# A row mean over 64 MB: the last row of each partition in three pieces instead of two

## The chip, the core and the metric

One core of a Trainium2 chip runs the kernel alone. The metric is the time of one execution on the device in microseconds (us); the median of the runs is what counts. Besides, one execution is recorded by the hardware profiler. Its span, from the first profiled instruction to the last, is a little shorter than the time, since some work lies around it.

The engines that matter here: VectorE (DVE), ScalarE (ACT) and GpSimd (POOL) compute; SyncE (SP) issues DMAs; 16 DMA engines move the data. A semaphore of a DMA is raised by each of the 16 engines, so a transfer counts as landed when the last of them is done.

## The reference

```python
def reference(x: np.ndarray, divisor: float) -> np.ndarray:
    return (np.sum(x, axis=-1) / divisor).astype(np.float32)
```

`x` is 32 x 512 x 1024 in float32 (67.1 MB), `divisor` is 1024. So 16384 rows of 1024 numbers are each summed and scaled by 1/1024.

## The kernel before

The 16384 rows lie on 128 partitions, 128 rows on each. They go in three groups: the first 16 rows of each partition (`x_first`), 96 rows (`x_main`), and the last 16 (`x_last`). Each load brings some rows of all partitions, one contiguous run per partition, and every load is issued from SP in the order of the program (`load`, L181, L182). The bulk loads of 14, 12 or 9 rows rotate through three buffers `t`, so a load waits until DVE has finished with the buffer it goes into.

- First and main group (L197 to L207): DVE sums the rows of a buffer in one reduction (L205). In the last two loads of the group ACT takes 4 and 5 of the rows (`act_sum`, L184 to L186). POOL then scales all sums (L207).
- Last group (L208 to L218): 9, 4 and 2 rows, in `t`, `t4` and `t2`. Here `dve_mean` (L188 to L195) is used: it adds the second half of a row to the first, scales, and accumulates the result along the row, in one pass of half the width. The accumulated value is written by a second small instruction, the accumulator read (DVE_READ_ACCUMULATOR2_ANT). ACT takes 4, 2 and 1 of these rows.
- The last row comes in two halves of 512 columns, `pa` and `pb` (L219, L220). `dve_mean` of `pa` (L226) writes its sum into column 512 of `pb`, behind the 512 columns that the DMA brings. Column 513 is zero: POOL clears columns 512 and 513 early (L179). `dve_mean` of `pb` (L227) then runs over 514 columns, that is 257 wide, takes the carried sum along, scales by 1/1024 and writes the last column of `fin`. So the second half waits for the first one's sum, through a semaphore of DVE itself, and for its own DMA.

The stores: `res0` (L223) and `res` (L224) are issued on SP behind all loads; `fin` (L228) last. Three functions work on the finished program. `start_loads_at_once` puts the loads that wait for nothing (the first three) ahead of the start barrier. `latest_wait_first` orders the waits of an instruction so that the wait for a DMA stays on the instruction itself, while the others become semaphore waits (EVENT_SEMAPHORE) of their own in front of it. `close_while_storing` moves the store of `fin` into the closing part of the program: it is issued once the last DVE result is there (semaphore `landed`), and the closing barrier of the engines runs while it is under way.

Each DMA counts on one of eight semaphores in turn, and its issue waits for the transfer that last used the same one.

Of the kernel before, what the change touches and what calls it, by code (L numbers as in the profile page):

```python
# [9 lines left out]
F32 = mybir.dt.float32  # L10
# [115 lines left out]
@with_exitstack  # L126
def kernel(
    ctx: ExitStack,
    tc: tile.TileContext,
    x: bass.AP,  # L130
    divisor: float,
    out: bass.AP,
):
    nc = tc.nc
    landed = nc.alloc_semaphore("landed")
    nc.at_finalize(start_loads_at_once)
    nc.at_finalize(latest_wait_first)
    nc.at_finalize(lambda nc: close_while_storing(nc, landed))
    xf = x.flatten_outer_dims()
    N, D = xf.shape  # L140
    P = nc.NUM_PARTITIONS
    scale = 1.0 / float(divisor)
    J = N // P
    assert J * P == N


    F, L = 16, 16
    M = J - F - L
    W = M + L
    x_first = bass.AP(tensor=x.tensor, offset=0, ap=[[F * D, P], [D, F], [1, D]])  # L150
    x_main = bass.AP(tensor=x.tensor, offset=P * F * D, ap=[[W * D, P], [D, M], [1, D]])
    x_last = bass.AP(tensor=x.tensor, offset=P * F * D + M * D, ap=[[W * D, P], [D, L], [1, D]])
    o_first = bass.AP(tensor=out.tensor, offset=0, ap=[[F, P], [1, F]])
    o_main = bass.AP(tensor=out.tensor, offset=P * F, ap=[[W, P], [1, M]])
    o_last = bass.AP(tensor=out.tensor, offset=P * F + M, ap=[[W, P], [1, L]])


    first = [(2, 0), (14, 0)]
    main = [(14, 0)] * 5 + [(14, 4), (12, 5)]
    last = [(9, 4), (4, 2), (2, 1)]  # L160
    assert sum(n for n, _ in first) == F
    assert sum(n for n, _ in main) == M and sum(n for n, _ in last) == L - 1

    pad = ctx.enter_context(tc.tile_pool(name="pad", bufs=1))
    pad.tile([P, 224], F32, name="pad")
    bulk = ctx.enter_context(tc.tile_pool(name="bulk", bufs=3))
    one = ctx.enter_context(tc.tile_pool(name="one", bufs=1))
    psum = ctx.enter_context(tc.tile_pool(name="junk", bufs=4, space=bass.MemoryType.PSUM))


    c = 512
    t4 = one.tile([P, 4, D], F32, name="t4")
    t2 = one.tile([P, 2, D], F32, name="t2")
    pa = one.tile([P, 768], F32, name="pa")[:, :c]
    pb = one.tile([P, D - c + 16], F32, name="pb")[:, : D - c + 2]
    res0 = one.tile([P, F], F32, name="res0")
    res = one.tile([P, M], F32, name="res")
    fin = one.tile([P, L], F32, name="fin")
    nc.gpsimd.memset(pb[:, D - c :], 0.0)  # L179

    def load(dst, src):  # L181
        tc.keep_in_program_order(nc.sync.dma_start(out=dst, in_=src))  # L182

    def act_sum(dst, src, by=1.0):  # L184
        junk = psum.tile([P, D], F32, name="junk")
        nc.scalar.activation(junk, src, COPY, scale=by, accum_out=dst)  # L186

    def dve_mean(dst, src, by=scale):  # L188


        h = src.shape[-1] // 2
        nc.vector.tensor_tensor_reduce(  # L192
            out=src[:, :h], in0=src[:, :h], in1=src[:, h:], scale=by, scalar=0.0,
            op0=ADD, op1=ADD, accum_out=dst,
        )  # L195

    for loads, src, dst in ((first, x_first, res0), (main, x_main, res)):  # L197
        j = 0
        for rows, on_act in loads:
            t = bulk.tile([P, 14, D], F32, name="t")  # L200
            load(t[:, :rows, :], src[:, j : j + rows, :])
            d = rows - on_act
            for i in range(d, rows):
                act_sum(dst[:, j + i : j + i + 1], t[:, i, :])
            nc.vector.reduce_sum(out=dst[:, j : j + d], in_=t[:, :d, :], axis=AX)  # L205
            j += rows
        nc.gpsimd.tensor_scalar_mul(out=dst, in0=dst, scalar1=scale)  # L207
    j = 0  # L208
    for rows, on_act in last:
        t = bulk.tile([P, 14, D], F32, name="t")[:, :rows, :] if rows > 4 else t4 if rows == 4 else t2  # L210
        load(t, x_last[:, j : j + rows, :])
        d = rows - on_act
        for i in range(rows):
            if i < d:
                dve_mean(fin[:, j + i : j + i + 1], t[:, i, :])
            else:
                act_sum(fin[:, j + i : j + i + 1], t[:, i, :], by=scale)
        j += rows  # L218
    load(pa, x_last[:, j, :c])  # L219
    load(pb[:, : D - c], x_last[:, j, c:])  # L220


    tc.keep_in_program_order(nc.sync.dma_start(out=o_first, in_=res0))  # L223
    tc.keep_in_program_order(nc.sync.dma_start(out=o_main, in_=res))  # L224

    dve_mean(pb[:, D - c : D - c + 1], pa, by=1.0)  # L226
    dve_mean(fin[:, j:], pb)  # L227
    tc.keep_in_program_order(nc.sync.dma_start(out=o_last, in_=fin))  # L228


# [33 lines left out]
```

## Time and profile before

| what | us |
|---|---|
| time, median of 3 runs | 160.5 (160.44 to 160.51) |
| span of the profiled execution | 159.0 |
| DVE busy | 117.2 |
| ACT busy | 18.5 |
| end of the load of `t2` (2 rows), by what waits for it | 155.86 |
| issue of the store of `fin` | 157.56 |

The span is the time between the first and the last profiled instruction. The kernel reads 67.11 MB, at 422 GB/s as a mean over the span. DVE waits 34.0 us in front of the reductions of L205, in each case for a DMA. "PEq", "SPq" and the like are an engine's sequencer, which waits, branches and issues while the engine itself does nothing.

### The profile page before, as it was taken

To read this page: it belongs to the slowest core of one execution; us is meant where nothing else is said; L and a number is where in the kernel's file an instruction comes from. 1 tells how busy PE (TensorE), PEld (TensorE's weight loads), DVE (VectorE), ACT (ScalarE), POOL (GpSimd) and SP (SyncE) were. 2 spreads that over 40 slices of the span, in tenths; PEclk is the share of its full clock that TensorE was granted. 3 is DMA by queue.
4 is the path that set the end of the run, shared out by engine and by line. 5 is a ranking of instruction groups with operands and counts; after the bars stand their busy time and mean duration, and the time that the engine had idled before them with its cause. 6 is when DMAs were issued, how large, how long until landed. Compare 5 with 4: busy or idle time off the path is not lost.

```text
span 159.0 us, 148 instructions
## 1 busy us (share of the span) xinstructions
DVE 117.2 (74%) x29; ACT 18.5 (12%) x33; POOL 1.0 (1%) x7
## 2 busy tenths in 40 slices
DVE  0500059995999599978999599959995996395643
ACT  3000000000000000000000000000000900390684
POOL 0000000000000000000000000000000000001000
DMA  7999999959999999699999999699999999999894
GB/s 278 447 462 462 462 462 462 462 260 433 462 462 462 462 462 462 303 390 462 462 462 462 462 462 404 303 447 462 462 462 429 396 396 408 482 445 445 350 420 169
DMA packets 2448, 67.18 MB, mean 422 GB/s; under 512 B 656, under 2 KB 656, under 8 KB 912
## 3 DMA queue, kind: packets, MB, share of 16 engines
q1 hardware_dynamic: 2448, 67.18, 98.3%
HBM read 67.11 MB, written 0.07 MB: 422 GB/s over the span
## 4 chain that ended last, share of the span: by engine, by line
DMA 77%; DVE 21%; SPq 1%; issue 0%; DVEq 0%
DMA t<-in_x_dram 56%; DMA pb<-in_x_dram 21%; DVE res L205 20%; SPq L182 1%; DVE pb L192 0%; DVEq L259 0%
## 5 line engine op out<-in xcount | busy, mean ns | idle before, releaser
L205 DVE TENSOR_REDUCE res<-t 128x14 f32<-128x14336 f32 (+3 forms) x9 | 111.2, 12360 | 34.0 <-DMA t<-in_x_dram 34.0
L186 ACT ACTIVATE junk<-t 128x1024 f32<-128x1024 f32 x16 | 16.2, 1013 | 136.8 <-DMA t<-in_x_dram 136.8
L192 DVE CUSTOM_DVE_ANT_0 t<-t 128x512 f32<-128x512 f32 x8 | 5.1, 688 | 6.1 <-DMA t<-in_x_dram 6.1
L186 ACT ACTIVATION_READ_ACCUMULATOR junk<-t 128x1 f32 x16 | 3.0, 186 | 0.0
L207 POOL TENSOR_SCALAR res<-res 128x16 f32<-128x16 f32 (+1 forms) x2 | 0.7, 352 | 143.3 <-DVE res L205 143.3
L186 ACT ACT_TABLE_LOAD x1 | 1.3, 1283 | 1.7 <-PEq L245 1.7
L192 DVE DVE_READ_ACCUMULATOR2_ANT fin<- 128x1 f32 x9 | 0.7, 82 | 0.0
L192 DVE CUSTOM_DVE_ANT_0 pb<-pb 128x257 f32<-128x257 f32 x1 | 0.4, 428 | 0.2 <-DMA pb<-in_x_dram 0.2
L192 DVE CUSTOM_DVE_ANT_0 pa<-pa 128x256 f32<-128x256 f32 x1 | 0.4, 426 | 0.0
L179 POOL MEMSET pb<- 128x2 f32 x1 | 0.1, 99 | 1.3 <-POOLq L245 1.3
L245 POOL MEMSET const-bfloat16-1.0<- 128x1 bf16 x1 | 0.1, 101 | 0.0
L245 POOL MEMSET const-uint8-127<- 128x1 uint8 x1 | 0.1, 101 | 0.0
L245 POOL MEMSET const-float32-0.0<- 128x1 f32 x1 | 0.1, 98 | 0.2 <-issue 0.2
L245 POOL MEMSET const-float32-1.0<- 128x1 f32 x1 | 0.1, 98 | 0.0
L192 DVE DVE_READ_ACCUMULATOR2_ANT pb<- 128x1 f32 x1 | 0.1, 84 | 0.0
## 6 DMA issues: line engine op xcount, KB each, us to landing
t<-in_x_dram SPq DMA_DIRECT2D x7, 7168.0 KB, 35.6
t<-in_x_dram SPq DMA_DIRECT2D x1, 6144.0 KB, 33.3
t<-in_x_dram SPq DMA_DIRECT2D x1, 4608.0 KB, 27.2
t<-in_x_dram SPq DMA_DIRECT2D x2, 1024.0 KB, 19.2
t<-in_x_dram SPq DMA_DIRECT2D x1, 2048.0 KB, 31.7
pa<-in_x_dram SPq DMA_DIRECT2D x1, 256.0 KB, 33.8
pb<-in_x_dram SPq DMA_DIRECT2D x1, 256.0 KB, 33.9
out_dram<-res SPq DMA_DIRECT2D x1, 48.0 KB, 11.6
```

Of the source, the lines that this page charges most:

```text
L179: nc.gpsimd.memset(pb[:, D - c :], 0.0)
L182: tc.keep_in_program_order(nc.sync.dma_start(out=dst, in_=src))
L186: nc.scalar.activation(junk, src, COPY, scale=by, accum_out=dst)
L192: nc.vector.tensor_tensor_reduce(out=src[:, :h], in0=src[:, :h], in1=src[:, h:], scale=by, scalar=0.0, op0=ADD, op1=ADD, accum_out=dst,)
L205: nc.vector.reduce_sum(out=dst[:, j : j + d], in_=t[:, :d, :], axis=AX)
L207: nc.gpsimd.tensor_scalar_mul(out=dst, in0=dst, scalar1=scale)
L245: nc = _bacc.Bacc("TRN2", target_bir_lowering=False, num_devices=1)
```

## The change

The last row comes in three loads, of 384, 352 and 288 columns (1536, 1408 and 1152 bytes per partition). `dve_mean` of a piece writes its sum behind the columns of the next one, so there are two carried sums instead of one. The widths on DVE become 192, 177 (half of 352 + 2) and 145 (half of 288 + 2). POOL clears two pairs of columns. The tiles are 2048 bytes per partition each, in place of one of 3072 and one of 2112; `t`, `t4` and `t2` keep their places.

```diff
-    c = 512
+    cuts = ((0, 384), (384, 736), (736, D))
     t4 = one.tile([P, 4, D], F32, name="t4")
     t2 = one.tile([P, 2, D], F32, name="t2")
-    pa = one.tile([P, 768], F32, name="pa")[:, :c]
-    pb = one.tile([P, D - c + 16], F32, name="pb")[:, : D - c + 2]
+    pieces = [
+        one.tile([P, 512], F32, name=f"piece{k}")[:, : hi - lo + 2 * (k > 0)]
+        for k, (lo, hi) in enumerate(cuts)
+    ]
...
-    nc.gpsimd.memset(pb[:, D - c :], 0.0)
+    for piece, (lo, hi) in zip(pieces[1:], cuts[1:]):
+        nc.gpsimd.memset(piece[:, hi - lo :], 0.0)
...
-    load(pa, x_last[:, j, :c])
-    load(pb[:, : D - c], x_last[:, j, c:])
+    for piece, (lo, hi) in zip(pieces, cuts):
+        load(piece[:, : hi - lo], x_last[:, j, lo:hi])
...
-    dve_mean(pb[:, D - c : D - c + 1], pa, by=1.0)
-    dve_mean(fin[:, j:], pb)
+    for piece, after, (lo, hi) in zip(pieces, pieces[1:], cuts[1:]):
+        dve_mean(after[:, hi - lo : hi - lo + 1], piece, by=1.0)
+    dve_mean(fin[:, j:], pieces[-1])
     tc.keep_in_program_order(nc.sync.dma_start(out=o_last, in_=fin))
```

In the built program the order of all other instructions is as before on every engine. DVE has one operation with its accumulator read more, and one more semaphore wait; the wait in front of the second piece is for POOL and DVE together, that in front of the third for DVE. On SP the third load stands between the second and the store of `res0`; the stores count on the next semaphores in turn, so the store of `fin` waits for the transfer of 9 rows instead of that of 12 rows.

## The prediction

> **What bounds the kernel now.** I read the page's chain of waits first, to see which work ends last.
>
> ```profile
> ## 4 chain that ended last, share of the span: by engine, by line
> DMA 77%; DVE 21%; SPq 1%; issue 0%; DVEq 0%
> DMA t<-in_x_dram 56%; DMA pb<-in_x_dram 21%; DVE res L205 20%; SPq L182 1%; DVE pb L192 0%; DVEq L259 0%
> ```
>
> The DMAs carry the span, and the last link of them is `pb`. The DVE share of 21% is no work that has to be shortened: those reductions free buffers while the loads already queued keep moving. The same chain in order of time shows where it ends:
>
> ```profile
> 122.59 0.04 issue
> 122.64 0.46 SPq L182
> 123.09 0.04 issue
> 123.14 33.94 DMA pb<-in_x_dram
> 157.08 0.02 issue
> 157.10 0.43 DVE pb L192
> 157.53 0.01 DVEq L259
> ```
>
> `pb` is issued at 123.14 and lands at 157.08, because it stands in the queue behind some 14 MB of other loads. What ends the kernel is therefore: last landing, one DVE operation, store. The timeline of that end (start, duration, engine, line):
>
> ```profile
> 155.86 0.69 DVE L192 CUSTOM_DVE_ANT_0 t<-t 128x512 f32<-128x512 f32 x1 [1.17 <-DMA t<-in_x_dram]
> 156.48 0.08 DVE L192 DVE_READ_ACCUMULATOR2_ANT fin<- 128x1 f32 x1
> 156.49 0.43 DVE L192 CUSTOM_DVE_ANT_0 pa<-pa 128x256 f32<-128x256 f32 x1
> 156.84 0.08 DVE L192 DVE_READ_ACCUMULATOR2_ANT pb<- 128x1 f32 x1
> 157.10 0.43 DVE L192 CUSTOM_DVE_ANT_0 pb<-pb 128x257 f32<-128x257 f32 x1 [0.17 <-DMA pb<-in_x_dram]
> 157.45 0.08 DVE L192 DVE_READ_ACCUMULATOR2_ANT fin<- 128x1 f32 x1
> 157.56 0.33 SPq L228 DMA_DIRECT2D out_dram<-fin  x1
> ```
>
> DVE is busy almost without a break from 155.86 on; it waits only 0.17 us for `pb`. That is all the slack there is for more DVE work in front of the last operation. From the issue of the store at 157.565 (the trace has these times to the nanosecond, and I use three digits from here on) to the end of the span at 159.002 it takes 1.437 us, and nothing in that part is changed. The engines' closing barrier ends at about 158.25, 0.7 us ahead of the landing of that store; a later DVE end moves both.
>
> **The change part by part.**
>
> *The DMA.* The trace's packet records give one packet per partition, 8 per DMA engine and transfer. On one engine, packets of 2048 bytes start every 80 ns, those of 8192 every 306 ns, those of 384 (the store of `res`) every 19 ns. The first two give 0.0367 ns per byte and 4.8 ns per packet; for 384 bytes that makes 18.9, as seen. Behind the 8 packets comes one of 4 bytes, 6 ns, for the semaphore. So the pieces take 8 x (61.2 + 56.5 + 47.1) + 3 x 6 = 1336 ns, where the halves took 2 x (8 x 80 + 6) = 1292: the row is 44 ns longer on the queue. The last semaphore packet of `t2` starts in the trace at 155.468, and a transfer is seen as landed 0.32 to 0.37 us after its last one. Hence the landings: piece 0 at about 156.32, piece 1 at 156.75 to 156.79, piece 2 at 157.12 (before: 156.471 and 157.078). Bounds: if nothing per packet is added, 157.08; if a packet under 2048 bytes cost the full 80 ns, 24 x 80 + 18 = 1938 ns, 157.72. The row of 384 bytes speaks clearly for the line through the three sizes, and I take 157.12.
>
> The Trainium skill has a rule against this cut ("DMA: Bandwidth & Descriptors", How a descriptor splits into AXI transactions): a run that does not start on a multiple of 256 bytes also fetches the bytes in front of it. Piece 2 starts at byte 2944 of a row, 11.5 x 256. By the rule it takes 40 beats of 32 bytes rather than 36, an estimate of 38 ns over 8 packets at the line's 0.0367 ns per byte. The store of `res` starts its runs at 448-byte steps, mostly off such a multiple, and its 19 ns show no surcharge. By the rule the last landing would be 157.16, and the sum below would not move.
>
> *Work removed and added on DVE.* From an operation's start to the start of its accumulator read there are 617 ns for width 512, 352 for 257 and 350 for 256: 1.043 ns per column and 83 ns fixed. So 283 ns for 192, 268 for 177, 234 for 145. The accumulator read takes 84 ns. Per row of 1024 that is one operation's fixed 83 ns and one read of 84 more, in exchange for a last operation that is 118 ns shorter.
>
> *The handover of the sum.* Operations that do not depend on each other follow closely: at 156.477 the read of the `t2` row starts, and the next operation could start at the same time (as the rows at 149.11 and 149.72 do). An operation that needs the sum of the one before must wait for the end of the read. For `pa` to `pb` this wait was hidden by the DMA, but its first part is in the trace: the read ended at 156.927, the semaphore wait of DVE for it started at 156.966 and took 21 ns. What then passes until an operation starts is not shown, since `pb` had not landed. Bounds: 0 ns at the least; at the most the 102 ns from the end of POOL's wait for the start barrier to its first MEMSET behind it. ACT shows 55 ns in the same place, up to its table load. I take 55: of the two, ACT is the one that works like DVE here (operation, then accumulator read), and both rows have a branch in between, which can only make them longer. So a handover costs 39 + 21 + 55 = 115 ns from the end of a read (60 to 162).
>
> *The sum on the path.* Piece 0 starts at 156.477 (DVE is free, the piece landed at 156.32); its read starts at 156.760 and ends at 156.844. Handover: piece 1 starts at 156.959; it landed 0.17 us earlier. Read from 157.227 to 157.311. Handover: piece 2 starts at 157.426; it landed at 157.12, 0.30 us earlier. Its read starts at 157.660. The store of `fin` followed the start of the last read by 112 ns (157.453 to 157.565): issue at 157.772 instead of 157.565. So **+0.207 us**, and written with the handover h: 2h - 0.023 us, +0.10 for h = 60 ns and +0.30 for h = 162 ns. The wait for the last DMA is gone from the end; what is late next is the chain of three operations on DVE, tied by two sums.
>
> The Trainium skill would price the handover lower ("VectorE: DVE Perf Modes", The DRAIN you can't avoid): a chain of copies took the same time with a semaphore after each as with one at the end. Here the next operation starts with the accumulator read and not behind it, so that a wait on the read has something to lose: 84 ns of it and the 39 ns that the trace shows. By the rule, with no price for the handover, piece 2 would wait for its landing and the store would go out at about 157.49, 0.07 us earlier than before.
>
> *What costs nothing.* POOL clears a second pair of columns, 99 ns at about 1.8 us; POOL's next work is at 36.7 and DVE needs the zeros at 156.5, so more than 30 us cover it; without them it would be those 99 ns. SP issues one load more, 0.48 us with the gap (123.136 to 123.620). Behind it stand the store of `res0`, which queues behind the pieces in any case, and that of `res`, which waits for POOL until 145.82: 21.6 us of SP's waiting hide it; without them, half a microsecond. The stores' waits for other DMA semaphores are for transfers that landed at 123.08, 137.62 and 148.47, each before the store is due. The two stores in the queue land 44 ns later, at 157.48 instead of 157.43, which the barrier's 0.7 us hide. No piece of the bulk loads or of their buffers moves.
>
> The span would be 159.00 + 0.21 = 159.21 us. The median of the runs stands 1.5 us above the span; I leave that as it is: 160.5 + 0.2 = **160.7 us**, 0.13% slower, which is inside the 0.2% (0.32 us) that a measurement of this kernel tells from no change.
>
> **The rivals.**
>
> *The landing still decides.* If the handover hides in the pipeline, the end is the landing at 157.12 + 0.02 + 0.234 + 0.112 = 157.49: -0.07 us, 160.43. For it: without a dependency the next operation does start with the read. Against it: the 39 ns behind the read's end are in the trace, and a wait on the read cannot end before it.
>
> *Slower: the handover is dearer than any row.* From h = 172 ns on, 2h - 0.023 passes 0.32 us. The place is the start of pieces 1 and 2 on DVE. With 250 ns, if an operation behind such a wait is made ready only after it, it makes +0.48 us, 160.98. For it: the wait is a separate instruction in front of the operation, and that of piece 1 asks for two semaphores (POOL's waits for two took 43 ns, for one 17). Against it: the dearest row, POOL's, gives 162 ns, with a branch inside.
>
> *Slower: small packets do not move by their bytes.* At 80 ns each, piece 2 lands at 157.72, its operation starts at 157.74, the store at 158.09: +0.52 us, 161.0. The 384-byte row speaks against it.
>
> *It doesn't do what it says.* Another mishap, or a gain through a part of the transfer I do not see, is left: the loads ahead are the same in size, order and place, so there is little for it.
>
> **How the numbers follow.** My forecast, the chain on DVE with the handover between its bounds (160.60 to 160.80): 0.66. The landing decides (about 160.43): 0.07. The dear handover (160.82 to 161.1): 0.17. Small packets (161.0): 0.06. A gain beyond all this, over 0.32 us: 0.04. The range for 8 in 10: the forecast's own, down to 160.50 and up to 160.90 for part of the dear handover. Faster by over 0.2%: 0.04; slower by over 0.2%: 0.17 + 0.06 and 0.02 of the forecast's edge, 0.25; within: 0.71.
>
> **What would show it.** In the profile after, the first of the three operations starts at 156.48 without idle time, the second about 0.12 us after the first one's read has ended, and the third likewise, and the chain of waits ends in DVE lines of two pieces instead of in a DMA. Last landing at 157.12; store of `fin` at 157.77. The forecast is wrong if the third operation waits for its DMA, if the gap behind a read is over 0.17 us or under 0.06, or if packets of 1152 bytes start more than some 50 ns apart on an engine.

## The result and the profile after

The changed kernel takes 161.06 us (median of 5 runs, 160.78 to 161.24), the kernel before beside it 160.50 (160.44 to 160.57). The ratio is 1.0031, 95% interval 1.0019 to 1.0043: slower by 0.3%, where the prediction had 160.7 and a range up to 160.9. In two later comparisons of the same two kernels (e1 and e8 below) the ratio is 1.0017, with intervals 1.0003 to 1.0030 and 1.0003 to 1.0031. Part of the first difference was therefore probably not the change, and most of what follows separates the two parts.

The profiled execution after has a span of 159.45 us (before 159.00). Its chain of waits, in order of time (start, duration, what):

```profile
156.76 0.28 DVE piece L195 x2
157.04 0.13 issue
157.17 0.36 DVE piece L195 x2
157.53 0.03 issue
157.56 0.02 DVEq L195
157.58 0.08 issue
157.66 0.31 DVE piece L195
157.98 0.01 DVEq L263
```

The DMA that ended the chain before is gone. In its place stand three DVE operations with two gaps of "issue" (in the second with "DVEq" between), in which DVE waits for no other engine and for no transfer, only for its own semaphore. The timeline of DVE and the store (start, duration, engine, line, operation):

```profile
156.06 0.69 DVE L195 CUSTOM_DVE_ANT_0 t<-t 128x512 f32<-128x512 f32 x1 [1.18 <-DMA t<-in_x_dram]
156.68 0.08 DVE L195 DVE_READ_ACCUMULATOR2_ANT fin<- 128x1 f32 x1
156.68 0.35 DVE L195 CUSTOM_DVE_ANT_0 piece<-piece 128x192 f32<-128x192 f32 x1
156.96 0.08 DVE L195 DVE_READ_ACCUMULATOR2_ANT piece<- 128x1 f32 x1
157.17 0.34 DVE L195 CUSTOM_DVE_ANT_0 piece<-piece 128x177 f32<-128x177 f32 x1
157.44 0.08 DVE L195 DVE_READ_ACCUMULATOR2_ANT piece<- 128x1 f32 x1
157.66 0.31 DVE L195 CUSTOM_DVE_ANT_0 piece<-piece 128x145 f32<-128x145 f32 x1
157.90 0.08 DVE L195 DVE_READ_ACCUMULATOR2_ANT fin<- 128x1 f32 x1
158.01 0.33 SPq L232 DMA_DIRECT2D out_dram<-fin  x1
```

Two measures divide the span here. The first is **T**, the start of the DVE operation on the `t2` row, which follows the landing of `t2` by 0.02 us. Everything ahead of it is the stream of bulk loads. The second is the **stretch** from T to the issue of the store of `fin`, which holds everything that the change touches. With the trace's nanoseconds:

| | before | after | difference |
|---|---|---|---|
| T | 155.860 | 156.059 | +0.199 |
| stretch | 1.705 | 1.952 | +0.247 |
| store to the end of the span | 1.437 | 1.437 | 0.000 |
| span | 159.002 | 159.448 | +0.446 |

The pieces landed at 156.54, 156.93 and 157.31. The operations on them started at 156.68, 157.17 and 157.66, so each of the pieces lay there 0.14 to 0.36 us before its operation. What the operations wait for is the sum: from the end of an accumulator read to the next operation there are 130 and 144 ns.

### The profile page after: what moved, and what is told of

It reads as the page before. It is cut to its first block, busy times and chain, and to the rows that moved or that the text cites. A ratio compares the mean times of both kernels' runs of the same rounds, so it can differ in the third digit from the quotient of the medians.

```text
span 159.4 us, 154 instructions
## 1 busy us (share of the span) xinstructions
DVE 117.4 (74%) x31; ACT 18.5 (12%) x33; POOL 1.0 (1%) x8
## 5 line engine op out<-in xcount | busy, mean ns | idle before, releaser
L195 DVE CUSTOM_DVE_ANT_0 piece<-piece 128x192 f32<-128x192 f32 (+2 forms) x3 | 1.0, 338 | 0.3
```

Of the source, the lines that this page charges most:

```text
L195: nc.vector.tensor_tensor_reduce(out=src[:, :h], in0=src[:, :h], in1=src[:, h:], scale=by, scalar=0.0, op0=ADD, op1=ADD, accum_out=dst,)
```

## The experiments

The stretch is read from one profile each and the ratio from timed runs beside the kernel before. Its median there was 160.63 (35 runs, beside e1 to e4), 160.71 (35 runs, beside e5 to e8) and 160.52 us (27 runs, beside e9 to e11), each of the three groups on another chip; over the 97 runs it is 160.62, the fastest and slowest 160.30 and 161.37.

**e1 and e8: the changed kernel, unaltered.**

> The changed kernel unaltered. Its first profile had the end of the kernel 0.25 us longer (from the start of the t2 row's DVE operation to the issue of the store of fin: 1.951 us against 1.705), and besides the landing of t2 0.20 us later, though nothing ahead of it was changed. Theory (the two handovers on DVE are the change's cost; the late landing comes and goes from run to run): the stretch is again 1.95 us within 0.02, the landing of t2 lies anywhere from 155.8 to 156.4 us, and the median is between 160.7 and 161.2 us. Rival (the change itself makes the earlier stream later): t2 lands at 156.0 us or later in every profile of the changed kernel, and before 155.9 in the profiles of kernels with two halves.

> The changed kernel once more beside before, for the size of the change. Theory (tail alone, the rest of the first difference was the stream's scatter): stretch 1.95 us within 0.02, the difference of the medians 0.25 us within 0.15, wherever t2 lands. Rival (the change costs 0.5 us): the difference is 0.4 us or more.

Stretch 1.953 and 1.952 us: the second and third profile of it agree with the first to 1 ns. T was 155.875 and 156.614. The median was 160.83 in e1 (160.59 to 161.53, 12 runs), 0.20 over before, and 161.09 in e8 (160.60 to 161.44, 12 runs), 0.38 over before, near the edge of what was expected; the ratio is 1.0017 in both, which is 0.27 us. The rival of e1 falls: T of 155.875 is nearly as early as in the first profile before, and e2 has a late T without the change.

**e2: the kernel before, unaltered.**

> The kernel before unaltered, as the null of the comparison. Theory of run to run variation: ratio 1.000 within 0.002, stretch from the t2 operation to the store 1.705 us within 0.02, and the time may vary by some tenths of a us among its runs on this chip, as the changed kernel's did. Rival (the change makes the stream late): all runs within 160.4 to 160.6 us and t2 landing before 155.9 us.

Stretch 1.710 us, T 156.255, ratio 1.0000 (0.9985 to 1.0014), single runs from 160.30 to 161.33 us. The old kernel can be late too. The 0.13 us over which its first 5 runs had spread was a calm sample.

**e4: two halves, result tiles where the changed kernel has them.**

```diff
-    pa = one.tile([P, 768], F32, name="pa")[:, :c]
-    pb = one.tile([P, D - c + 16], F32, name="pb")[:, : D - c + 2]
+    pa = one.tile([P, 512], F32, name="pa")[:, :c]
+    pb = one.tile([P, 1024], F32, name="pb")[:, : D - c + 2]
```

> Two halves as before, in tiles of 2048 and 4096 bytes, so that res0, res and fin lie at the places that they have in the changed kernel. Theory: as before, ratio 1.000 within 0.002, stretch 1.705 us. Rival (the place of the result tiles in SBUF makes the stream late): t2 lands at 156.0 us or later and the ratio is 1.001 or more.

Stretch 1.703 us, T 155.932, ratio 0.9995 (0.9981 to 1.0009). So the places of the tiles show no effect on the stretch, on T or on the time.

**e3: three pieces, one handover.**

```diff
-        one.tile([P, 512], F32, name=f"piece{k}")[:, : hi - lo + 2 * (k > 0)]
+        one.tile([P, 512], F32, name=f"piece{k}")[:, : hi - lo + 2 * (k == 2)]
...
-    for piece, (lo, hi) in zip(pieces[1:], cuts[1:]):
-        nc.gpsimd.memset(piece[:, hi - lo :], 0.0)
...
-    for piece, after, (lo, hi) in zip(pieces, pieces[1:], cuts[1:]):
-        dve_mean(after[:, hi - lo : hi - lo + 1], piece, by=1.0)
+    w = cuts[2][1] - cuts[2][0]
+    for k in range(2):
+        dve_mean(pieces[2][:, w + k : w + k + 1], pieces[k], by=1.0)
```

The two sums fill both columns behind piece 2, so POOL clears nothing here, and the waits for POOL are gone too. Piece 1 is 176 wide on DVE instead of 177.

> Three pieces, but the sums of pieces 0 and 1 both go behind the columns of piece 2, so piece 1 doesn't wait for the sum of piece 0 and only one handover is on the path. Theory (each handover costs about 0.13 to 0.14 us behind the end of an accumulator read, the read's 0.08 us included it is 0.22): piece 1's operation starts with the accumulator read of piece 0, the stretch from the t2 operation to the store is 1.95 - 0.21 = 1.74 us within 0.03, and the median is 0.2 us below that of the changed kernel in this call. Rival (the third load and the third operation as such are the cost, not the sum carried between them): the stretch stays at 1.9 us or more.

Stretch 1.742 us; median 160.67, ratio 1.0002 (0.9989 to 1.0016), 0.16 us under the median of e1, which ran beside it. The timeline of its DVE:

```profile
156.95 0.08 DVE L193 DVE_READ_ACCUMULATOR2_ANT piece<- 128x1 f32 x1
156.95 0.34 DVE L193 CUSTOM_DVE_ANT_0 piece<-piece 128x176 f32<-128x176 f32 x1
157.22 0.08 DVE L193 DVE_READ_ACCUMULATOR2_ANT piece<- 128x1 f32 x1
157.45 0.31 DVE L193 CUSTOM_DVE_ANT_0 piece<-piece 128x145 f32<-128x145 f32 x1
```

The second piece's operation now starts at 156.95, together with the first one's read; only the last one still stands off, 0.144 us behind the read's end. Loads and operations are as many as in the changed kernel, and 0.21 of its 0.247 us are gone.

**e5 and e6: four pieces of 256 columns, three handovers or one.** e5 is the changed kernel with other cuts; e6 has those cuts and all three sums behind the last piece, which has four columns more, cleared at once by POOL. The line of `cuts` holds for both, what stands behind the dots for e6 alone.

```diff
-    cuts = ((0, 384), (384, 736), (736, D))
+    cuts = ((0, 256), (256, 512), (512, 768), (768, D))
...
-    for piece, after, (lo, hi) in zip(pieces, pieces[1:], cuts[1:]):
-        dve_mean(after[:, hi - lo : hi - lo + 1], piece, by=1.0)
+    for k in range(3):
+        dve_mean(pieces[3][:, w + k : w + k + 1], pieces[k], by=1.0)
```

> Four pieces of 256 columns, each sum carried into the next: three handovers on the path. Theory (every exposed handover costs 0.084 us of accumulator read and 0.13 to 0.14 us behind it): from the start of the t2 operation 0.617 us, then four operations of 0.217 to 0.218 us up to their reads, three times 0.084 + 0.137 us, and 0.112 us to the store: stretch 2.26 us within 0.03, 0.31 us over the three chained pieces; the median 0.5 to 0.6 us over before. Rival (loads and operations cost, not the carried sum): the stretch grows by one operation alone, 0.08 us over the three pieces, and equals that of e6.

> The same four pieces, but the first three sums all go behind the columns of the last one: one handover on the path. Theory: 0.617 + 3 x 0.217 + 0.084 + 0.137 + 0.219 + 0.112 = 1.82 us for the stretch within 0.03, 0.44 us less than e5 with the same loads, the same number of operations and the same bytes; the median 0.1 us over before. Rival (loads and operations cost): no difference between e5 and e6 beyond 0.03 us.

Stretch 2.251 us in e5 and 1.814 in e6, medians 161.22 and 160.76, ratios 1.0028 (1.0014 to 1.0041) and 1.0006 (0.9990 to 1.0022). In e5 the starts of the chained operations lie 0.43 to 0.45 us apart:

```profile
156.88 0.08 DVE L195 DVE_READ_ACCUMULATOR2_ANT piece<- 128x1 f32 x1
157.09 0.29 DVE L195 CUSTOM_DVE_ANT_0 piece<-piece 128x129 f32<-128x129 f32 x1
157.31 0.08 DVE L195 DVE_READ_ACCUMULATOR2_ANT piece<- 128x1 f32 x1
157.53 0.29 DVE L195 CUSTOM_DVE_ANT_0 piece<-piece 128x129 f32<-128x129 f32 x1
```

In e6 operations of nearly that size, which carry nothing into each other, lie 0.21 us apart, and only the last one stands off:

```profile
156.98 0.08 DVE L195 DVE_READ_ACCUMULATOR2_ANT piece<- 128x1 f32 x1
156.98 0.29 DVE L195 CUSTOM_DVE_ANT_0 piece<-piece 128x128 f32<-128x128 f32 x1
157.19 0.08 DVE L195 DVE_READ_ACCUMULATOR2_ANT piece<- 128x1 f32 x1
157.19 0.29 DVE L195 CUSTOM_DVE_ANT_0 piece<-piece 128x128 f32<-128x128 f32 x1
157.41 0.09 DVE L195 DVE_READ_ACCUMULATOR2_ANT piece<- 128x1 f32 x1
157.63 0.29 DVE L195 CUSTOM_DVE_ANT_0 piece<-piece 128x130 f32<-128x130 f32 x1
```

Two handovers less are worth 2.251 - 1.814 = 0.437 us, 0.22 each, at the same loads, bytes and number of operations. The rival, that loads and operations are the cost, has fallen.

**e7: two pieces, of 640 and 384 columns.**

```diff
-    c = 512
+    c = 640
```

> Two pieces only, 640 and 384 columns: as many loads and operations as before, a shorter last operation, and the handover is no longer hidden, as the first piece lands later and takes longer. Theory: pa lands 0.77 us after the start of the t2 operation, its read starts 0.417 us later, 0.084 + 0.137 us for the handover, 0.284 us up to the last read, 0.112 us: stretch 1.83 us within 0.04, 0.12 us over before. Rival (a shorter last piece is what counts and the handover hides): the operation starts with the landing at 1.29 us and the stretch is 1.69 us.

Stretch 1.837 us; median 160.87, ratio 1.0004 (0.9988 to 1.0021), too small a step for the timed runs. `pb` landed at 157.23 and its operation started at 157.45, 0.145 us behind the end of the read of `pa`:

```profile
157.22 0.08 DVE L192 DVE_READ_ACCUMULATOR2_ANT pb<- 128x1 f32 x1
157.45 0.36 DVE L192 CUSTOM_DVE_ANT_0 pb<-pb 128x193 f32<-128x193 f32 x1
```

So two pieces pay the price as well as soon as nothing covers it, and a third load has no part in it.

**e9: the changed kernel with the waits exchanged.** An operation here carries one wait itself; a second one becomes a wait of its own in front of it. In the kernels so far the wait for the landing stands on the operation and that for the sum in front. In the traces the exchange touches the operations of the last row alone.

```diff
     def rank(i, w):
...
+        if w.ant_name.startswith("DVE_") and i.engine == DVE and w.wait_value > 7:
+            return -1
         if w.ant_name.startswith("DMAHW") and i.engine != SP:
             return 0
```

> The changed kernel with the two waits of pieces 1 and 2 exchanged: the wait for the carried sum, which ends last, stands on the operation itself, the wait for the landing becomes the separate one in front. Theory (of the 0.137 us behind the read's end some 0.04 us is the way of the semaphore, and the remaining 0.1 us is the separate wait and the start of the operation behind it): both handovers shrink to about 0.04 to 0.06 us, stretch 1.78 us within 0.04, 0.17 us less than the changed kernel with the same loads and operations. Rival (0.137 us is the engine's own price for reading what it has just written): the stretch stays 1.95 us within 0.03.

Stretch 1.745 us, 0.207 less than the changed kernel; median 160.59, ratio 1.0005 (0.9996 to 1.0013). The timeline:

```profile
157.03 0.08 DVE L197 DVE_READ_ACCUMULATOR2_ANT piece<- 128x1 f32 x1
157.15 0.34 DVE L197 CUSTOM_DVE_ANT_0 piece<-piece 128x177 f32<-128x177 f32 x1
157.41 0.08 DVE L197 DVE_READ_ACCUMULATOR2_ANT piece<- 128x1 f32 x1
157.53 0.31 DVE L197 CUSTOM_DVE_ANT_0 piece<-piece 128x145 f32<-128x145 f32 x1
```

From a read's end to the next operation there are now 35 and 34 ns (before the exchange 130 and 144). Those 35 are what the sum still costs behind the read; the rest was the form of the wait.

**e10: the same exchange in the kernel before.**

> The reverse test on the kernel before: there the landing of pb ends last, and the exchange puts the separate wait on it. Theory: the last operation starts some 0.1 us later behind the landing, stretch 1.81 us within 0.03 instead of 1.705. Rival (the engine's own price for the sum, not the form of the wait): stretch 1.705 us within 0.02, as the sum is there in time either way.

Stretch 1.810 us; median 160.55, ratio 1.0004 (0.9992 to 1.0016). The timeline:

```profile
157.02 0.08 DVE L194 DVE_READ_ACCUMULATOR2_ANT pb<- 128x1 f32 x1
157.37 0.43 DVE L194 CUSTOM_DVE_ANT_0 pb<-pb 128x257 f32<-128x257 f32 x1 [0.27 <-DMA pb<-in_x_dram]
```

`pb` landed at 157.234 and the operation started 134 ns later, where 23 ns pass in the kernel before. The separate wait costs its 0.1 us on whichever event comes last.

**e11: e3 with the waits exchanged.**

> e3 (both sums into the last piece) with the exchanged waits. Here sum and landing come within 0.05 us of each other, so the theory expects little: the separate wait ends with the landing at 1.26 to 1.28 us, the operation can start 0.1 us behind it, stretch 1.72 us within 0.04 (e3 1.742). A stretch of 1.66 us or less would be below that of before and a version to build on; the rival (the engine's own price) expects 1.74.

Stretch 1.740 us, ratio 0.9996 (0.9985 to 1.0007). Theory and rival expected nearly the same and this run tells nothing between them. It shows no way past the kernel before: sum and landing come within 0.05 us of each other, and one of the two has to stand in the separate wait. None of the kernels has a shorter stretch than the 1.70 to 1.71 us of two equal halves.

## Why the prediction missed

**What bounds the end: right.** DVE became the chain that ends last, tied by two sums; the third operation did not wait for its DMA. None of the three signs of being wrong that the prediction named came up. The rival in which the landing still decides fell: the handover does not hide. The Trainium skill's statement, measured on a chain of copies, that a semaphore between VectorE operations costs nothing ("VectorE: DVE Perf Modes", The DRAIN you can't avoid) does not carry over to this pair of operation and accumulator read: e5 against e6 measures 0.22 us for each.

**The DMA: right.** Landings relative to T were forecast at 0.46, 0.89 to 0.93 and 1.26 us and measured at 0.48, 0.87 and 1.25. On the first DMA engine to finish, the 8 packets of 1152 bytes and the 6 ns behind them took 383 ns, as the line through the sizes had it, so a packet took 47.1 ns. The rival of 80 ns each fell, and so did, for these packets, the surcharge of the rule on runs that do not start on a multiple of 256 bytes ("DMA: Bandwidth & Descriptors", How a descriptor splits into AXI transactions): it would have given 421. The starts of pieces 0 and 1 lie 128 bytes off that of piece 2 in steps of 256, and their packets took the line's time as well (61.2 and 56.4 ns), so the place of the tensor itself hides no surcharge. The store of `res`, which the prediction set against that rule, doesn't bear on it: its 448-byte steps are places that it writes, and the rule is one for reading.

**The operations: right.** The reads started 280, 269 and 235 ns behind the operations (forecast 283, 268, 234), and the store 112 ns behind the last read (112).

**The handover: right in kind, short in size.** It was put at 39 + 21 + 55 = 115 ns behind the read. It measured 130 and 144 in the changed kernel. The term that was too small is the 55 ns, taken from ACT's start behind the barrier: where the separate wait can be seen, it ends 60 ns behind the read, and 84 more pass. The prediction held that a branch made ACT's row too long, if anything; no row of the trace shows that branch, and 84 is more than 55. For the same reason the 0.17 us for which DVE waited for `pb` were no free slack: with 84 ns behind the wait that ended at 156.987, the sum would have let the operation start at 157.071, 30 ns before it did. Two equal halves only just hid the handover in this profile. The sum on the path was +0.247 us instead of +0.207. That alone would have put 160.75 against 160.5, inside the range. The measured 161.06 lies where the rival of a dear handover had put it, yet that rival fell as well: it needed 172 ns or more, and the wait for two semaphores, which was its argument, gave the shorter of the two gaps.

**The step that failed is the one from the span to the time:** "The median of the runs stands 1.5 us above the span; I leave that as it is: 160.5 + 0.2". It adds the growth of the stretch to a median of three runs that lay within 0.07 us, and it takes the end of the bulk loads as fixed ("No piece of the bulk loads or of their buffers moves"). Their scatter from run to run is put at nothing, in the sum and in the range up to 160.9.

What the runs showed in its place is a T that scatters by 0.75 us over the 13 profiles, with and without the change. In the 12 later profiles the time of the profiled execution itself stood 1.32 to 1.34 us above its span. By that the first profile before, with its 159.00, belongs to an execution of 160.33 us, faster than all 5 runs of the first comparison; its T of 155.86 is the earliest of all. The first comparison had 161.06 - 160.50 = 0.56 us, of which the stretch explains 0.247 and leaves 0.31. Of its five changed runs only the fastest, 160.78, was profiled, with T 0.20 us later than in the first profile before; that T was later still in the others is inferred, since no other part of the span or of the time above it varied by more than 0.02 us in profiles of the same kernel.

That the 0.31 us fell to the changed kernel's side is luck, as far as these runs tell: the repeats gave ratios worth 0.27 us, and 0.247 us on top of the median of 160.62 of the 97 later runs of before would be 160.87, inside the range. That T is not tied to the change is seen in e1 (changed, early) and e2 (unchanged, late); the intervals of the repeats, 0.05 to 0.50 us, do not exclude a shift of T by the change of up to 0.2 us either way. Why the 5 runs of before were all calm and those after were not, the runs don't show.

## What to carry to other kernels

A reduction that is cut into pieces to shorten its tail pays for every exposed carried sum; let the pieces write their sums side by side into the last one, so that only one handover is left, and compare the total with what the transfer had covered before. Where an instruction has two waits, the one that ends last belongs on the instruction itself: here that was worth 0.1 us per handover (e9), and the wrong order cost as much (e10). For a change of 0.2 us, read the stretch that it touches in several profiles, and don't take three agreeing runs for the scatter of the whole.

## What the runs showed of the hardware

The handover on DVE has three parts: the accumulator read, 81 to 85 ns; 35 ns from its end to the next operation when the wait stands on the operation itself (e9); and, if the wait is a separate instruction, 95 to 110 ns more. A separate wait for two semaphores at once was the cheaper one: 130 or 131 ns behind the read, in each of its five profiled cases of e1, e5, e8 and the changed kernel, against 144 or 145 for a separate wait for one semaphore.

The largest delays of T come with slow packets of the bulk loads. Most packets of 57344 bytes take 2116 ns; single ones take up to 2364. The excess over 2116 ns, summed over all such packets and divided by the 16 engines, goes with T (correlation 0.89 over the 13 profiles, of kernels of both kinds):

| profile | excess, us | T, us |
|---|---|---|
| before | 0.09 | 155.860 |
| e1 (changed) | 0.15 | 155.875 |
| e4 (two halves) | 0.20 | 155.932 |
| e7 (640 and 384) | 0.14 | 156.011 |
| e10 (two halves) | 0.08 | 156.021 |
| e5 (four pieces) | 0.17 | 156.049 |
| e3 (three pieces) | 0.16 | 156.051 |
| after | 0.26 | 156.059 |
| e9 (changed, waits exchanged) | 0.07 | 156.133 |
| e6 (four pieces) | 0.25 | 156.152 |
| e2 (before) | 0.54 | 156.255 |
| e11 (three pieces) | 0.50 | 156.314 |
| e8 (changed) | 0.78 | 156.614 |

The correlation rests on the three latest (0.26 over the other ten); e9 and e10 have as little excess as the profile before and are still 0.27 and 0.16 us later. In e10 the first load lands 0.27 us later (4.88 against 4.61). In e9 0.22 us more than in the profile before come between the landings of the loads of 12 and of 9 rows, and the packets of the latter, 36864 bytes and 1364 ns each before, take up to 1589.

Of the 459 packets of 57344 bytes that took over 2140 ns in all 13 profiles, 277 start in the first 53 us; in the three latest (e2, e8, e11) many lie in the middle third of the span. What slows them is not in the trace, and it wasn't tried.
